# SBUF homes moved by small steps under a stream of float32r matmuls

## The chip, the cores and the metric

The kernel runs on one core of one Trainium2 chip. The metric is the device time of one execution in microseconds (us), the median of several runs. A profile of one execution stands beside it. The engines are called as the profile calls them: PE is the matrix engine (TensorE), PEld its weight loads, DVE the vector engine, ACT the scalar engine, POOL the general engine (GpSimd) and SP the queue that issues most transfers. SBUF is the on-chip memory: 128 partitions, and a tile's home is its byte offset, the same in all of them.

## The reference, cut to what matters

A residual of 256 tokens by 2048 features passes through five phases. Each takes `rms_norm(x) * gain`, multiplies it by weight matrices, does something in between, and adds the product of a last matrix to the residual:

```
x += mixer(norm(x))        # w_in [2048, 8272], gated recurrence + sparse attention, w_out [2048, 2048]
x += cross(norm(x), mem)   # wq, wk, wv [2048, 512], attention over 256 memory rows, wo [512, 2048]
x += relu(norm(x) @ w_up)**2 @ w_down          # w_up [2048, 8192], w_down [8192, 2048]
x += neighbourhood(norm(x))                    # w_qkv [2048, 6144], w_o [2048, 2048]
x += relu(norm(x) @ w1)**2 @ w2                # w1 [2048, 8192], w2 [8192, 2048]
```

All in float32. Some 440 MB of weights are each used once for the 256 tokens.

## The kernel before, in words

The program is one stream of weight chunks with side work beside it. A chunk is at most 1024 float32 columns in each partition: two 128-row tiles of a 512-column block (four of a 256-column block). For each, SP brings a `raw` tile (512 KB, `emit_dma`), ACT copies it to `hi` in float32r (L374), and DVE writes the rest, `raw - hi`, to `lo` (L375). Activations are split in two the same way. A product of two split numbers takes three matmuls: high by high, high by low, low by high. That is `emit_mm`, which has two forms:

- Transposed blocks (`tr=True`, line L408): the weights stand still (128 columns of `hi` or `lo`) and the activations stream past, 256 columns of `xT_hi` or `xT_lo`. These are the indexer's, gates' and up-projection blocks.
- Token blocks (L415, L416, L417): 128 columns of activations stand still and the weights stream past, 512 columns (256 for the value projection of the cross attention). The standing operand is `xT_hi`, `xT_lo` for projections of the residual, or a region tile (`r0` to `r8`) for projections of something made in between: squared-ReLU activations, attention outputs, the normalised memory rows.

```
nc.tensor.matmul(dst, h, wh, start=first, stop=False)   # L415: h, l stand still; wh, wl stream
nc.tensor.matmul(dst, h, wl, start=False, stop=False)   # L416
nc.tensor.matmul(dst, l, wh, start=False, stop=last)    # L417
```

The standing operand is always the second of the tiles that the program names for a matmul, and the streaming one the first: `acc<-hi,r` streams `hi` past a region tile. The order of all work is written out when the program is made: estimated clocks (`spend`, `Paced`) decide when a stage of side work goes between two chunks. They depend on operand sizes and not on homes.

Homes follow from the order in which the pools were opened (`const`, `stream`, `reg`, `tmp`, `small`) and from the tile sizes. Before the change: a scratch of 16384 bytes for the descriptors of POOL's transfers, four constants of 32 bytes each that the toolchain places, then `cst` 1024, `band` 256, `lvl` 896, `gT` 512, `X` 16384 bytes; so `xT_hi` and `xT_lo` (16384 bytes each) begin at 256 modulo 512. Small tiles after them add up so that `stream` begins at 32 modulo 512. Everything in `stream` (4 `raw`, 4 `hi`, 4 `lo` of 4096 bytes) and in `reg` (nine regions of 8192 bytes) has a size that is a multiple of 512, so all of these, and the wide working tiles in `tmp`, begin at 32 modulo 512. All slices that matmuls of the stream take begin at multiples of 512 bytes inside their tiles, except in one 80-column block.

Of the kernel before, what the change touches and what calls it, by code (L numbers as in the profile page):

```python
# [12 lines left out]
F32 = mybir.dt.float32  # L13
F32R = mybir.dt.float32r
# [8 lines left out]
P = 128  # L23
T = 256
# [9 lines left out]

# columns of the transposed table of gains
G_MIX, G_CROSS, G_MEM, G_MLP, G_MIX2, G_MLP2 = 0, 16, 32, 48, 64, 80
# [19 lines left out]
class Block:  # L56
    """One block of output columns: w[kts, cols] against the stationary activations."""

# [6 lines left out]
class Act:  # L65
    """Transposed activations, each value split exactly into two float32r parts."""

# [8 lines left out]
def block_kernel(ctx: ExitStack, tc: "_tile.TileContext", a: dict, out: bass.AP, phases=ALL_PHASES):  # L76
# [27 lines left out]
    def region(i, shape, dtype=F32):  # L104
        return reg.tile(shape, dtype, tag=f"r{i}", name=nm(f"r{i}"))

    # ------------------------------------------------------------------ lanes of side work
    # Work beside the stream of weights is written as generators, each in a lane. The estimated clocks
    # below only order the program: a stage goes out when the one before it should be done by the time
    # the tensor engine gets there, and when ACT and DVE aren't too far behind it.  # L110
    clock = {"pe": 0.0, "act": 0.0, "dve": 0.0, "pool": 0.0}
# [100 lines left out]

    # ------------------------------------------------------------------ constants
    cst = const.tile([P, 2 * P], F32, name="cst")
# [3 lines left out]
    gT = const.tile([P, P], F32, name="gT")  # L218
    X = const.tile([P, 2, D], F32, name="X")
    xT_hi = const.tile([P, KT, T], F32R, name="xT_hi")  # L220
    xT_lo = const.tile([P, KT, T], F32R, name="xT_lo")
# [10 lines left out]

    # ------------------------------------------------------------------ small arithmetic
    def rsqrt(lane, x, n, mul=1.0, out=None):
        """1/sqrt(x) * mul of a [P, n] tile: an integer first guess, then Newton's steps."""
        g = st(f"rg{lane}", n, I32)
        vec.tensor_scalar(g, x.bitcast(I32), 1, None, op0=ALU.logical_shift_right)
        vec.tensor_scalar(g, g, -1, RSQRT_MAGIC, op0=ALU.mult, op1=ALU.add)
        y = st(f"ry{lane}", n) if out is None else out
        h = st(f"rh{lane}", n)  # L240
        for i in range(3):
            y0 = g.bitcast(F32) if i == 0 else y
            m = mul if i == 2 else 1.0
            gps.tensor_tensor(h, y0, y0, op=ALU.mult)
            gps.tensor_tensor(h, h, x, op=ALU.mult)
            gps.tensor_scalar(h, h, -0.5 * m, 1.5 * m, op0=ALU.mult, op1=ALU.add)
            gps.tensor_tensor(y, h, y0, op=ALU.mult)
        return y
# [4 lines left out]
    def make_rstd(lane, key, ss, want_sq=False):  # L253
        """ss: [P, 2 * 4] sums of squares, one per token half and column block."""
        v = vec
        m = st(f"mr{lane}", 2)
        v.tensor_reduce(m, ss.rearrange("p (t c) -> p t c", t=2), axis=AX.X, op=ALU.add)
        ms = const.tile([P, 2], F32, name=nm("ms"))
        v.tensor_scalar(ms, m, 1.0 / D, EPS, op0=ALU.mult, op1=ALU.add)
        if want_sq:  # L260
            r2 = const.tile([P, 2], F32, name=nm("rsq"))
            v.reciprocal(r2, ms)
            rstd_sq[key] = r2
        else:
            rstd[key] = rsqrt(lane, ms, 2, out=const.tile([P, 2], F32, name=nm("rstd")))
        mark(("rstd", key))
# [3 lines left out]
    def build_half(lane, ver, cb, gain, half):  # L270
        """Two feature tiles of the finished residual: transposed, with the gain, split in two."""
        yield from wait_for(("x", ver, cb))
        act = acts[ver]
        ps = sd("E")
        for j in range(2):
            kt = cb * 4 + half * 2 + j
            for tt in range(2):
                pe.transpose(
                    ps[:, j * T + tt * P : j * T + (tt + 1) * P], X[:, tt, kt * P : (kt + 1) * P], ident
                )  # L280
        yield
        for j in range(2):
            kt = cb * 4 + half * 2 + j
            act.put(kt, xT_hi[:, kt, :], xT_lo[:, kt, :])
        kts = [cb * 4 + half * 2 + j for j in range(2)]
        split_gains([act.parts[kt] for kt in kts], ps, [gcol(gain + kt) for kt in kts])
        for kt in kts:
            mark(("act", id(act), kt))
        yield
# [25 lines left out]
    def split_act(hi, lo, src, scale=None):  # L315
        """hi + lo = src * scale, exactly; src in PSUM or SBUF."""
        if scale is None:
# [8 lines left out]
    def product(dst, l, r, first=True, last=True):  # L326
        """dst (+)= l^T r; operands split in two parts take three products."""
        if not isinstance(l, tuple):
# [9 lines left out]
    def split_gains(parts, ps, gains):  # L338
        """The same of two feature tiles in one PSUM bank, each with its own gain."""
        srcs = [ps[:, j * T : (j + 1) * T] for j in range(2)]  # L340
# [4 lines left out]

    # ------------------------------------------------------------------ the stream of weights
    plan = []
# [22 lines left out]
    def emit_split(c):  # L370
        n = len(c.kts) * c.block.width
        c.hi = stream.tile([P, 1024], F32R, tag="hi", name=nm("hi"))
        c.lo = stream.tile([P, 1024], F32R, tag="lo", name=nm("lo"))
        nc.scalar.activation(c.hi[:, :n], c.raw[:, :n], AF.Copy)  # L374
# [51 lines left out]

    # ------------------------------------------------------------------ evacuations
    def ev_tokens(dst, key, after=None):
        """dst[tt] = projection * rstd, one row per token."""
        def ev(b):  # L430
# [12 lines left out]
    def ev_heads(dstT, key, gain, after, mul=1.0, lane="E", factor=None):  # L443
        """Four heads of 128: RMS norm of each, transposed; dstT(pair) is [128, 2, 256].

        With factor, the norm is left to the scores: factor["ss"] holds the heads' sums of squares.
        """
        def ev(b):
# [60 lines left out]
    def softmax_rows(lane, groups, factor=None):  # L509
        """groups: (scores [P, n, w] in SBUF or PSUM, destination [P, n, w]); normalised rows.  # L510

        factor(group) is a [P, n] of positive factors that the scores still lack.
        """
        v = vec
# [70 lines left out]

    # ------------------------------------------------------------------ phase: mixer
    def mixer():
# [45 lines left out]

        # --- indexer
        iqT = region(0, [P, 8, T])
# [89 lines left out]

        # --- sparse attention heads
        qT = region(2, [P, 8, T])
# [68 lines left out]

        # --- gated recurrence heads
        hold = {}
# [77 lines left out]
        def levels(g, pl):  # L876
            """Scores of the recurrence, S^T[s, t] = sum_k q[t] k[s] prod(f, s < . <= t): pairs are met at
            the level where a block of 2b tokens holds s in its left and t in its right half; q carries the
            products from its half's start, k those to its half's end."""
            v = vec  # L880
# [46 lines left out]
            def right_pairs(b, ps):  # L927
                """The level's products, for the tokens in right halves alone."""
                for i in range(2):
# [93 lines left out]

    # ------------------------------------------------------------------ attention of dense heads
    def probs_pair(qT, kTt, h0, pT, keys, bias=None, lane="A", pl="A", factor=None):
        """Two heads: softmax(q k^T + bias), transposed into the two tiles pT()."""
        yield from wait_for(*keys)
# [41 lines left out]
    def values_pair(pT, V, vcol, oT_hi, oT_lo, oh, act_o, vkey):  # L1069
        """out^T of two heads from their transposed probabilities, split into the next operand."""  # L1070
        yield from wait_for(vkey)
# [12 lines left out]

    # ------------------------------------------------------------------ phase: cross attention
    def cross():
# [96 lines left out]

    # ------------------------------------------------------------------ phase: squared-ReLU MLP
    def mlp(phase, w1, w2):
# [45 lines left out]

    # ------------------------------------------------------------------ phase: neighbourhood attention
    def na():
# [83 lines left out]

    # ------------------------------------------------------------------ the program
    warm = st("warm", 8)
# [106 lines left out]
```

## Time and profile before

| | |
|---|---|
| median of 3 runs | 2477.0 us (2476.63 to 2477.68) |
| profiled execution, first to last instruction | 2475.9 us |
| PE busy | 2459.3 us, 99% of the span |
| PE weight loads busy | 2186.8 us, 88% |
| DVE, ACT, POOL busy | 1455.8, 1136.8, 169.5 us |
| moved by transfers | 449.40 MB, mean 182 GB/s |

The span is the time from the first to the last instruction of the profiled execution; the 1.1 us between it and the median lie around it. PE's instructions overlap one another in the profile (the recorded length of one is longer than the distance to the next), so what one matmul costs is read from the distance between starts, not from its length.

### The profile page before, as it was taken

How to read it: one execution, taken by the hardware profiler on the slowest of the kernel's cores; microseconds unless marked ns; L12 is line 12 of the kernel's file. 1: busy time of each engine (PE TensorE's matmuls, PEld its weight loads, DVE VectorE, ACT ScalarE, POOL GpSimd, SP SyncE). 2: the span in 40 equal slices, each digit the busy share in tenths (PEclk: the TensorE clock that was granted, in tenths of full speed). 3: DMA queues.
4: the chain of work that ended last, by engine and by line, in shares of the span. 5: the costliest groups of instructions: out<-in, count | busy, mean ns of one | idle time of the engine just before them, and what ended most of it. 6: DMA issues, size and time to landing. Idle time of an engine off the chain costs nothing.

```text
span 2475.9 us, 36932 instructions
## 1 busy us (share of the span) xinstructions
PE 2459.3 (99%) x14885; PEld 2186.8 (88%) x14885; DVE 1455.8 (59%) x1719; ACT 1136.8 (46%) x1465; POOL 169.5 (7%) x345
## 2 busy tenths in 40 slices
PE   8999999999999999999999999999999999999999
PEld 8779998888998899899898888888998899899897
DVE  5575666665655555555556566666655555555554
ACT  5455533465543444444444554554543444444443
POOL 1020012211000000000000312230000000000000
PEclk9999999999999999999999999999999999999999
DMA  7555545555556556566655656555556656566654
GB/s 225 162 172 161 151 145 156 193 177 167 170 178 198 193 182 194 187 194 191 189 187 174 196 169 179 167 186 180 179 180 195 195 180 196 188 194 188 190 187 167
DMA packets 235644, 449.40 MB, mean 182 GB/s; under 512 B 16321, under 2 KB 21057, under 8 KB 235473
## 3 DMA queue, kind: packets, MB, share of 16 engines
q1 hardware_dynamic: 232528, 440.19, 57.0%
q0 software_dynamic: 2368, 5.80, 1.0%
q8 instruction: 116, 1.90, 0.3%
q10 hardware_dynamic: 576, 1.05, 0.1%
q14 instruction: 56, 0.45, 0.1%
HBM read 444.83 MB, written 2.10 MB: 181 GB/s over the span
## 4 chain that ended last, share of the span: by engine, by line
PE 95%; POOL 1%; DMA 1%; DVE 1%; ACT 1%; issue 0%; SPq 0%; ACTq 0%; POOLq 0%; DVEq 0%
PE acc L408 34%; PE acc L415 19%; PE acc L416 19%; PE acc L417 19%; PE sdA L157 3%; PE sdE L157 2%; DMA raw<-in_w_in_dram 1%; DMA relraw<-in_rel_dram 0%; POOL rhB L157 0%; ACT hi L374 0%; DVE lo L375 0%; DMA wA<-in_mem_dram 0%; POOL rhD L157 0%; DVE wB L157 0%; POOL rhE L157 0%
## 5 line engine op out<-in xcount | busy, mean ns | idle before, releaser
L375 DVE TENSOR_TENSOR lo<-raw,hi 128x1024 fp32r<-128x1024 f32 (+1 forms) x835 | 1005.1, 1222 | 495.0 <-ACT hi L374 492.0
L374 ACT ACTIVATE hi<-raw 128x1024 fp32r<-128x1024 f32 (+1 forms) x835 | 867.7, 1056 | 799.5 <-PE acc L417 406.0
L408 PE MATMUL acc<-xT_hi,hi 128*128 128x256 f32 x2448 | 690.6, 282 | 0.0
L408 PE MATMUL acc<-xT_hi,lo 128*128 128x256 f32 x2448 | 688.3, 281 | 0.1
L408 PE MATMUL acc<-xT_lo,hi 128*128 128x256 f32 x2448 | 688.2, 281 | 0.0
L415 PE MATMUL acc<-hi,r 128*128 128x512 f32 (+1 forms) x1408 | 543.6, 386 | 0.7 <-ACT r L157 0.7
L417 PE MATMUL acc<-hi,r 128*128 128x512 f32 (+1 forms) x1408 | 541.5, 385 | 0.0
L416 PE MATMUL acc<-lo,r 128*128 128x512 f32 (+1 forms) x1408 | 541.4, 384 | 0.0
L408 PEld LDWEIGHTS acc<-xT_lo,hi 128*128 128x128 f32 x2448 | 461.2, 188 | 0.6
L408 PEld LDWEIGHTS acc<-xT_hi,hi 128*128 128x128 f32 x2448 | 461.2, 188 | 0.6
L408 PEld LDWEIGHTS acc<-xT_hi,lo 128*128 128x128 f32 x2448 | 461.2, 188 | 0.3 <-DVE lo L375 0.3
L417 PEld LDWEIGHTS acc<-hi,r 128*128 128x128 f32 x1408 | 264.5, 188 | 53.1 <-DVE r L157 0.4
L415 PEld LDWEIGHTS acc<-hi,r 128*128 128x128 f32 x1408 | 264.7, 188 | 52.3 <-ACT r L157 1.1
L416 PEld LDWEIGHTS acc<-lo,r 128*128 128x128 f32 x1408 | 264.7, 188 | 51.0
L415 PE MATMUL acc<-hi,xT_hi 128*128 128x512 f32 x736 | 295.0, 401 | 0.0
L416 PE MATMUL acc<-lo,xT_hi 128*128 128x512 f32 x736 | 290.9, 395 | 1.4 <-DVE lo L375 1.4
L417 PE MATMUL acc<-hi,xT_lo 128*128 128x512 f32 x736 | 290.5, 395 | 0.0
L157 DVE SCALAR_TENSOR_TENSOR X<-acc,rsq,X 128x512 f32<-128x512 f32 x128 | 96.1, 751 | 147.0 <-PE acc L417 147.0
L415 PEld LDWEIGHTS acc<-hi,xT_hi 128*128 128x128 f32 x736 | 138.1, 188 | 33.8 <-issue 2.7
L417 PEld LDWEIGHTS acc<-hi,xT_lo 128*128 128x128 f32 x736 | 137.9, 187 | 33.7
L416 PEld LDWEIGHTS acc<-lo,xT_hi 128*128 128x128 f32 x736 | 138.2, 188 | 32.7 <-DVE lo L375 1.9
L157 DVE SCALAR_TENSOR_TENSOR wE<-acc,wE 128x512 f32<-128x512 f32 x64 | 44.3, 692 | 109.2 <-ACT wE L157 108.6
(175 smaller groups left out, 1121.9 us busy)
## 6 DMA issues: line engine op xcount, KB each, us to landing
raw<-in_mlp_w_dram SPq DMA_DIRECT2D x256, 512.0 KB, 4.2
raw<-in_w_up_dram SPq DMA_DIRECT2D x128, 512.0 KB, 3.9
raw<-in_w_down_dram SPq DMA_DIRECT2D x128, 512.0 KB, 4.3
raw<-in_w_in_dram SPq DMA_DIRECT2D x127, 512.0 KB, 3.9
raw<-in_na_w_qkv_dram SPq DMA_DIRECT2D x96, 512.0 KB, 4.2
raw<-in_w_out_dram SPq DMA_DIRECT2D x32, 512.0 KB, 4.2
raw<-in_na_w_o_dram SPq DMA_DIRECT2D x32, 512.0 KB, 4.1
raw<-in_wk_x_dram SPq DMA_DIRECT2D x8, 512.0 KB, 4.4
```

Source lines behind the costliest of these rows:

```text
L157: return f(*args, **kw)
L374: nc.scalar.activation(c.hi[:, :n], c.raw[:, :n], AF.Copy)
L375: nc.vector.tensor_tensor(c.lo[:, :n], c.raw[:, :n], c.hi[:, :n], op=ALU.subtract)
L408: nc.tensor.matmul(dst, l, r, start=first and i == 0 and o == 0, stop=last and i == 2, skip_group_check=True,)
L415: nc.tensor.matmul(dst, h, wh, start=first, stop=False)
L416: nc.tensor.matmul(dst, h, wl, start=False, stop=False)
L417: nc.tensor.matmul(dst, l, wh, start=False, stop=last)
```

## The change: what it does

Four edits move homes; no instruction is added, taken away or reordered, and no operand changes its size.

- A tile of 32 bytes, `shift`, is put ahead of `xT_hi`.
- `hi` and `lo` tiles take 4160 bytes in place of 4096; the 1024 columns in use stay the same.
- Region `i` takes 8192 + 32 * i bytes; the part in use is a view on its first bytes.
- The descriptor scratch of POOL's transfers is 8192 bytes in place of 16384.

Beside them comments are dropped.

Modulo 512 bytes, the homes become:

| tile | before | after |
|---|---|---|
| `xT_hi`, `xT_lo` | 256 | 288 |
| `raw` | 32 | 64 |
| `hi`, four buffers | 32 | 64, 128, 192, 256 |
| `lo`, four buffers | 32 | 320, 384, 448, 0 |
| regions r0, r2, r3, r1, r4, r5, r8, r6, r7 (order of first use) | 32 | 64, 64, 128, 224, 256, 384, 32, 288, 480 |
| wide working tiles (`wA`, `wE`, `wB`) | 32 | 192 |

```diff
     def region(i, shape, dtype=F32):
-        return reg.tile(shape, dtype, tag=f"r{i}", name=nm(f"r{i}"))
+
+        flat = reg.tile([P, 2048 + 8 * i], dtype, tag=f"r{i}", name=nm(f"r{i}"))
+        n = 1
+        for d in shape[1:]:
+            n *= d
+        names = "abc"[: len(shape) - 1]
+        return flat[:, :n].rearrange(
+            f"p ({' '.join(names)}) -> p {' '.join(names)}", **dict(zip(names, shape[1:])))
...
     X = const.tile([P, 2, D], F32, name="X")
+    const.tile([P, 8], F32, name="shift")
     xT_hi = const.tile([P, KT, T], F32R, name="xT_hi")
...
-        c.hi = stream.tile([P, 1024], F32R, tag="hi", name=nm("hi"))
-        c.lo = stream.tile([P, 1024], F32R, tag="lo", name=nm("lo"))
+        c.hi = stream.tile([P, 1040], F32R, tag="hi", name=nm("hi"))
+        c.lo = stream.tile([P, 1040], F32R, tag="lo", name=nm("lo"))
...
-    nc = _bacc.Bacc("TRN2", target_bir_lowering=False, num_devices=1)
+    nc = _bacc.Bacc("TRN2", target_bir_lowering=False, num_devices=1, dynamic_dma_scratch_size=8192)
```

## Rows read from the trace of the kernel before

**Rows 1.** The page: busy time, share of the span and instructions of each engine.

```profile
PE 2459.3 (99%) x14885; PEld 2186.8 (88%) x14885; DVE 1455.8 (59%) x1719; ACT 1136.8 (46%) x1465; POOL 169.5 (7%) x345
```

**Rows 2.** The page: granted clock of PE in 40 slices, in tenths.

```profile
PEclk9999999999999999999999999999999999999999
```

**Rows 3.** The page: the chain that ended last, by engine, then by line.

```profile
PE 95%; POOL 1%; DMA 1%; DVE 1%; ACT 1%; issue 0%; SPq 0%; ACTq 0%; POOLq 0%; DVEq 0%
PE acc L408 34%; PE acc L415 19%; PE acc L416 19%; PE acc L417 19%; PE sdA L157 3%; PE sdE L157 2%; DMA raw<-in_w_in_dram 1%; DMA relraw<-in_rel_dram 0%; POOL rhB L157 0%; ACT hi L374 0%; DVE lo L375 0%; DMA wA<-in_mem_dram 0%; POOL rhD L157 0%; DVE wB L157 0%; POOL rhE L157 0%
```

**Rows 4.** Waits of PE: us in total, times, longest us.

```profile
PE sdE L157 <- DMA cst<-in_cst_dram: 2.9, 1, 2.9
PE sdA L157 <- DVE wA L157: 2.5, 3, 1.3
...
PE acc L416 <- DVE lo L375: 1.4, 1, 1.4
```

**Rows 5.** Groups of PE's instructions by form: count | busy us, mean ns of one.

```profile
L408 PE MATMUL acc<-xT_hi,hi 128*128 128x256 f32 x2432 | 686.2, 282 | 0.0
...
L415 PE MATMUL acc<-hi,r 128*128 128x512 f32 x1344 | 525.3, 391 | 0.7 <-ACT r L157 0.7
...
L415 PE MATMUL acc<-hi,xT_hi 128*128 128x512 f32 x736 | 295.0, 401 | 0.0
...
L415 PE MATMUL acc<-hi,r 128*128 128x256 f32 x64 | 18.3, 285 | 0.0
```

**Rows 6.** The chain, 860 to 1240 us: start us, us, what, how many.

```profile
869.62 45.44 PE acc L408 x384
...
958.62 45.44 PE acc L408 x384
...
1047.63 45.44 PE acc L408 x384
```

**Rows 7.** Timeline of PE, a token run of the first MLP: start us, us, instruction.

```profile
1003.90 0.40 PE L415 MATMUL acc<-hi,r 128*128 128x512 f32 x1
...
1005.99 0.39 PE L415 MATMUL acc<-hi,r 128*128 128x512 f32 x1
...
1006.67 0.39 PE L415 MATMUL acc<-hi,r 128*128 128x512 f32 x1
...
1047.24 0.39 PE L417 MATMUL acc<-hi,r 128*128 128x512 f32 x1
1047.47 0.28 PE L408 MATMUL acc<-xT_hi,hi 128*128 128x256 f32 x1
```

**Rows 8.** Timeline of PE, a token run of the neighbourhood projection.

```profile
1399.08 0.39 PE L416 MATMUL acc<-lo,xT_hi 128*128 128x512 f32 x1
...
1421.00 0.39 PE L417 MATMUL acc<-hi,xT_lo 128*128 128x512 f32 x1
```

**Rows 9.** Timeline of PE, the value projection of the cross attention.

```profile
592.05 0.28 PE L415 MATMUL acc<-hi,r 128*128 128x256 f32 x1
...
596.37 0.28 PE L415 MATMUL acc<-hi,r 128*128 128x256 f32 x1
```

**Rows 10.** Timeline of all engines at 1030 us: a matmul and the load beside it.

```profile
1030.02 0.39 PE L416 MATMUL acc<-lo,r 128*128 128x512 f32 x1
1030.02 0.19 PEld L417 LDWEIGHTS acc<-hi,r 128*128 128x128 f32 x1
```

**Rows 11.** The same at 1410 us.

```profile
1410.04 0.40 PE L415 MATMUL acc<-hi,xT_hi 128*128 128x512 f32 x1
1410.04 0.19 PEld L416 LDWEIGHTS acc<-lo,xT_hi 128*128 128x128 f32 x1
```

**Rows 12.** The view of transfers: issues, KB each, median us to landing.

```profile
relraw<-in_rel_dram POOLq DMA_DIRECT2D x32, 96.0 KB, 3.8
```

**Rows 13.** The chain, 1538 to 1560 us.

```profile
1544.60 0.61 POOL relraw L1272
1545.21 3.95 DMA relraw<-in_rel_dram
```

**Rows 14.** The page: the two split instructions, mean ns of one | idle before.

```profile
L375 DVE TENSOR_TENSOR lo<-raw,hi 128x1024 fp32r<-128x1024 f32 (+1 forms) x835 | 1005.1, 1222 | 495.0 <-ACT hi L374 492.0
L374 ACT ACTIVATE hi<-raw 128x1024 fp32r<-128x1024 f32 (+1 forms) x835 | 867.7, 1056 | 799.5 <-PE acc L417 406.0
```

## The prediction, made before the changed kernel was run

> **What bounds the kernel now.** I read the page first. PE is busy for 99% of the span [rows 1], at a granted clock that stays at the full level, 2.4 GHz, from the first slice to the last [rows 2]. The chain of work that ended last puts 95% on PE, and 91% on the four lines of the weight stream [rows 3]. The waits of PE agree: the longest is 2.9 us, for the first transfer of all, and the stream's longest is one of 1.4 us for a `lo` tile [rows 4]. So nothing but the distance from one matmul to the next sets the time, and the reader is to look at that distance alone.
>
> A table of groups can't show it: the mean lengths there (282, 391, 401 ns) run on under the next matmul [rows 5]. It has to be taken from stretches in which nothing comes between. There are four kinds, by shape and by where the two operands live:
>
> - Transposed, 256 columns of `xT` at 256 modulo 512 past weights at 32: 384 in 45.44 us, 118.3 ns each [rows 6].
> - Token, 512 columns of weights at 32 past region tiles at 32: from 1006.67 to 1047.24 us are 179 steps, 226.65 ns each. The first nine of the run, from 1003.90 to 1005.99, take 232 ns each; the run of 192 as a whole (1003.90 to 1047.47) 226.9 [rows 7].
> - Token, 512 columns of weights at 32 past `xT` at 256: 94 steps in 21.92 us, 233.2 ns each [rows 8].
> - Token, 256 columns of weights at 32 past region tiles at 32: 36 steps in 4.32 us, 120.0 ns [rows 9].
>
> Two things are to be seen. The second and the fourth kind differ only in columns, and 106.65 ns for 256 more columns is 0.4166 ns a column, one per tick of 2.4 GHz. So each matmul costs its columns and a toll: 226.65 - 213.3 = 13.3 ns, 120.0 - 106.7 = 13.3 ns, and by the same reckoning 233.2 - 213.3 = 19.9 ns for the third kind and 118.3 - 106.7 = 11.7 ns for the first. And the second and third kind have one shape, one count of weight loads (the next matmul's load begins with the matmul, [rows 10, 11]) and one engine clock, and yet stand 6.5 ns apart. What differs is which tiles meet: homes that are equal modulo 512 in the one, 224 apart in the other. The transposed run takes 45.44 us to the hundredth, three times out of three [rows 6], while ACT, DVE and the transfers fall on it differently each time; so the toll isn't made by them.
>
> The counts are 3 x 2432 transposed and 48 narrower ones like them (7,344), 3 x 1344 = 4,032 token with regions, 3 x 736 = 2,208 token with `xT`, and 3 x 64 = 192 narrow ones [rows 5]. The whole toll is 7,344 x 11.7 + 4,032 x 13.6 + 2,208 x 19.9 + 192 x 13.3 = 86 + 55 + 44 + 3 = 188 us, 13.6 ns per matmul, 7.6% of the span. That is the pot from which this change can take, and to which it can add: 1 ns of mean toll is 13.8 us.
>
> **The change part by part.** The 32-byte tile, the 64 bytes on each `hi` and `lo` and the 32 * i on each region issue nothing. Operands keep their shapes and the program its order, so instruction counts, waits and queues stay. What moves is which homes meet while a matmul streams and the next one's operand is loaded. Before, a meeting has one distance modulo 512 in each kind of run: 0, 224, or 288 for the transposed. After, the distance changes with each buffer: transposed runs meet at 288, 352, 416, 480 (with `hi`) and 32, 96, 160, 224 (with `lo`); the token runs with `xT` at the same set mirrored; those with regions at distances that depend on region and buffer. Of the region meetings, the equal homes that are now the rule become the exception: going through the four pairs of the MLP (r0 r1, r2 r3, r4 r5, r6 r7) against four `hi` and four `lo`, one in seven is still 0. And no run settles: a chunk has 12 token matmuls, and the run of rows 7 needed nine to fall from 232 to 226.65.
>
> The trace of before shows two distances for 512 columns and two for 256, and nothing of the others. So each kind is bounded by the two rows of its shape, and I take the middle, since the new distances lie on no row. Token with regions: bounds 226.65 and 233.2, middle 230.0; 4,032 x (230.0 - 226.9) = +12.5 us. Token with `xT`: the same middle; 2,208 x (230.0 - 233.2) = -7.1 us. Transposed: bounds 118.3 and 120.0, middle 119.15; 7,344 x 0.85 = +6.2 us. The narrow ones: 192 x (119.15 - 120.0) = -0.2 us. The sum is +11.4 us. With every kind at its lower row it is -1.0 - 14.5 + 0 - 0.3 = -16 us, at its upper row +25.4 + 0 + 12.5 + 0 = +38 us.
>
> The Trainium skill has a rule against any effect: the page "TensorE: Matmul & The Clock Gate", section "Step-by-step: what each phase is for", says that the streaming operand and the weight load have a read port each, so that loading the next tile's weights takes nothing from the running matmul. By it the sum would be 0; the trace here disagrees in so far as one shape runs at 226.65 and at 233.2 ns. The same page's section "Back-to-back issue gap" puts a lone warm matmul at N/2.4 + 2.5 ns, 215.8 and 109.2 here; if the whole toll above that went, an estimate by that page would be 150 us less, 2327 us, which no row here shows.
>
> The other parts cost nothing in the sum. ACT's copy and DVE's subtraction keep shapes and take 1,056 and 1,222 ns of the 2.7 us that 12 token matmuls last; they sit idle 800 and 495 us before these instructions [rows 14], so a few per cent on them is hidden. The smaller descriptor scratch touches POOL's queue alone: its main load is 32 bias transfers that land in 3.8 us [rows 12]. They lie on the chain in one place [rows 13]; should a later one have to wait there for an earlier landing, it is 3.95 us once, and elsewhere PE's stream covers it. I take 0.
>
> **The rivals.**
>
> *Separation pays.* Nine regions and eight stream buffers on their own offsets might keep the two readers out of each other's way, and the toll falls in every kind at once. For it: the toll does depend on the homes, and the kind with 224 between its homes pays the most, so some distances must be worse than others and a mixture of many need not be worse than today's. Against it: today's equal homes are the cheap case at 512 columns. Priced at the lowest toll of any row, 11.7 ns: 512 columns take 225.0 ns; 4,032 x (225.0 - 226.9) + 2,208 x (225.0 - 233.2) = -7.7 - 18.1 = -26 us, 2451 us. It decides as soon as the mean toll after falls under 13.6 ns; a toll 1 ns lower than any row gives another -14 us.
>
> *Nothing happens.* The homes modulo 512 aren't what sets the toll (the two token kinds also differ in which tiles they read and how far apart these are as a whole), and the new homes pay what the old did: 2477 us. For it: rows 7 and 8 are two points, no more. Against it: each kind would have to keep its own pace under a new distance.
>
> *Every meeting as dear as the dearest.* The 19.9 ns of rows 8 become the rule, for 256 columns too: 4,032 x 6.3 + 7,344 x 8.3 = 25 + 61 = +86 us, 2563 us. Against it: the transposed kind has a distance of 288, which is 224 the other way round, and pays only 11.7 ns.
>
> **How the numbers follow.** The sum is made against the span of 2475.9 us; the median of the runs, 2477.0, is 1.1 us more, and I set 11.4 on the median: 2488 us, slower by 0.5%. A measurement of this kernel can tell about 0.2%, 5 us, from no change. I give the forecast 0.40 (its own range 2482 to 2515), separation 0.36 (2430 to 2472), nothing 0.17, the dear case 0.07. So faster 0.36, no change 0.17, slower 0.47. The range from 2442 to 2512 leaves out the dear case, the last of the forecast's upper bound, and separation where it goes below 9 us under its price.
>
> **What the profile after would show.** PE's share and count stay; the chain stays on the stream's lines. The transposed runs of 384 take 45.8 us if the forecast is right, 45.44 or less under separation. The token run of 192 that took 43.57 us takes 44.2 us, and loses the even beat of 226 and 227 ns: a beat that changes from chunk to chunk, with the buffer. The token runs with `xT` become the one kind that is quicker, near 230 ns. I am wrong if the token runs with regions stay at or below 226.65 ns with their homes no longer equal: then equal homes were no advantage, and the sign of the sum turns on the transposed kind, half of all matmuls, for which the trace has only two rows 1.7 ns apart.

## The result: slower by 0.8%, all of it in the token runs with regions

| | before | after |
|---|---|---|
| median | 2476.8 us (2475.2 to 2477.7, 4 runs) | 2494.8 us (2494.1 to 2495.3, 4 runs) |
| ratio | | 1.0076, 95% interval 1.0064 to 1.0088 |
| profiled span | 2475.9 us | 2492.3 us |
| PE busy | 2459.3 us | 2477.6 us |

The page of the changed kernel has the same engines at the same work: instruction counts are equal, and the busy time of DVE, ACT and POOL moves by at most 1.5 us [rows 1 for before].

```profile
PE 2477.6 (99%) x14885; PEld 2186.4 (88%) x14885; DVE 1457.3 (58%) x1719; ACT 1136.4 (46%) x1465; POOL 169.8 (7%) x345
```

PE's busy time grew by 18.3 us, and its idle time (span less busy) fell from 16.6 to 14.7 us. So it is the pace of PE's matmuls again. The chain of the changed kernel, two of the 384-matmul transposed runs (start us, us, what), answers to [rows 6]:

```profile
782.29 45.37 PE acc L416 x384
872.14 45.32 PE acc L416 x384
```

They are a shade quicker than the 45.44 us of before: 118.0 to 118.1 ns in place of 118.3. (Line numbers have moved: L416 is the old L408, L423 to L425 are the old L415 to L417.) The timeline of PE in the changed kernel, first the token run of 192 that answers to [rows 7], from its first matmul to the next transposed one, then the run with `xT` of [rows 8]:

```profile
1007.26 0.40 PE L423 MATMUL acc<-hi,r 128*128 128x512 f32 x1
...
1051.83 0.28 PE L416 MATMUL acc<-xT_hi,hi 128*128 128x256 f32 x1
...
1407.15 0.39 PE L424 MATMUL acc<-lo,xT_hi 128*128 128x512 f32 x1
...
1429.09 0.39 PE L425 MATMUL acc<-hi,xT_lo 128*128 128x512 f32 x1
```

The first takes 44.57 us where it took 43.57: 232.1 ns a matmul in place of 226.9. The second takes 21.94 us for 94 steps, 233.4 ns, where it took 233.2. Multiplied out over the counts of [rows 5]: regions 4,032 x 5.2 = +21.0 us, `xT` 2,208 x 0.2 = +0.4 us, transposed 7,344 x -0.25 = -1.8 us, in all +19.6, against the 18.3 us that PE's busy time grew. The stretches shown speak for the whole: over all neighbouring matmuls of a kind in the two traces, the mean distance between starts goes from 227.6 to 232.7 ns with regions, from 236.1 to 235.9 with `xT`, and from 118.8 to 118.6 in the transposed kind.

POOL's smaller scratch cost nothing that can be seen. The waits of POOL in the changed kernel (us in total, times, longest) have its bias tiles waiting 43.4 us for their transfers; PE waits for none of them.

```profile
POOL relb L164 <- DMA relraw<-in_rel_dram: 43.4, 14, 4.8
```

### The profile page after: what moved, and what is told of

It reads as the page before. It is cut to its first block, busy times and chain, and to the rows that moved or that the text cites. A ratio compares the mean times of both kernels' runs of the same rounds, so it can differ in the third digit from the quotient of the medians.

```text
span 2492.3 us, 36932 instructions
## 1 busy us (share of the span) xinstructions
PE 2477.6 (99%) x14885; PEld 2186.4 (88%) x14885; DVE 1457.3 (58%) x1719; ACT 1136.4 (46%) x1465; POOL 169.8 (7%) x345
## 4 chain that ended last, share of the span: by engine, by line
PE 95%; POOL 1%; DVE 1%; ACT 1%; DMA 1%; issue 0%; SPq 0%; ACTq 0%; POOLq 0%; DVEq 0%
PE acc L416 33%; PE acc L423 19%; PE acc L425 19%; PE acc L424 19%; PE sdA L164 3%; PE sdE L164 2%; DMA raw<-in_w_in_dram 1%; DMA relraw<-in_rel_dram 0%; POOL rhB L164 0%; ACT hi L382 0%; DVE lo L383 0%; POOL rhD L164 0%; DVE wB L164 0%; DVE wA L164 0%; POOL rhE L164 0%
## 5 line engine op out<-in xcount | busy, mean ns | idle before, releaser
L416 PE MATMUL acc<-xT_hi,hi 128*128 128x256 f32 x2448 | 689.6, 282 | 0.0
L416 PE MATMUL acc<-xT_hi,lo 128*128 128x256 f32 x2448 | 687.8, 281 | 0.0
L416 PE MATMUL acc<-xT_lo,hi 128*128 128x256 f32 x2448 | 686.0, 280 | 0.0
L423 PE MATMUL acc<-hi,r 128*128 128x512 f32 (+1 forms) x1408 | 550.6, 391 | 0.7 <-ACT r L164 0.7
L424 PE MATMUL acc<-lo,r 128*128 128x512 f32 (+1 forms) x1408 | 547.7, 389 | 0.0
L425 PE MATMUL acc<-hi,r 128*128 128x512 f32 (+1 forms) x1408 | 547.6, 389 | 0.0
L416 PEld LDWEIGHTS acc<-xT_lo,hi 128*128 128x128 f32 x2448 | 461.5, 189 | 0.7
L416 PEld LDWEIGHTS acc<-xT_hi,hi 128*128 128x128 f32 x2448 | 460.4, 188 | 0.7
L416 PEld LDWEIGHTS acc<-xT_hi,lo 128*128 128x128 f32 x2448 | 459.9, 188 | 0.3 <-DVE lo L383 0.2
L425 PEld LDWEIGHTS acc<-hi,r 128*128 128x128 f32 x1408 | 264.6, 188 | 60.2 <-DVE r L164 0.4
L423 PEld LDWEIGHTS acc<-hi,r 128*128 128x128 f32 x1408 | 264.6, 188 | 58.5 <-ACT r L164 1.1
L423 PE MATMUL acc<-hi,xT_hi 128*128 128x512 f32 x736 | 295.3, 401 | 0.0
L425 PE MATMUL acc<-hi,xT_lo 128*128 128x512 f32 x736 | 291.1, 396 | 0.0
L423 PEld LDWEIGHTS acc<-hi,xT_hi 128*128 128x128 f32 x736 | 138.4, 188 | 33.5 <-issue 2.7
L425 PEld LDWEIGHTS acc<-hi,xT_lo 128*128 128x128 f32 x736 | 138.2, 188 | 33.5
```

The source lines that it names most:

```text
L416: nc.tensor.matmul(dst, l, r, start=first and i == 0 and o == 0, stop=last and i == 2, skip_group_check=True,)
```

## The experiments

Four theories are told apart. Theory 1: the distance between the home of the tile that stands still and that of the tile that streams sets the toll; in form a, the cheap beat needs one distance throughout, and only equal homes have it; in form b, it is the rotation of buffers that spoils it; in form c, only the distance modulo 256 counts, and it may alternate. Theory 2: each home's own alignment sets the toll. A distance below is the standing home less the streaming home, modulo 512 bytes. All of these kernels have the smaller scratch as well.

### The tile of 32 bytes and the smaller scratch alone

```diff
+    const.tile([P, 8], F32, name="pad_x")
     xT_hi = const.tile([P, KT, T], F32R, name="xT_hi")
...
+    nc = _bacc.Bacc("TRN2", target_bir_lowering=False, num_devices=1, dynamic_dma_scratch_size=8192)
```

> The kernel before with the 32-byte tile ahead of xT_hi and the smaller descriptor scratch alone: xT goes to 288, weight buffers and regions all to 64 modulo 512, so every distance between homes that meet is what it was. Theory 1 (the distance and its constancy set the toll): every kind of run keeps its pace (118.3, 226.65, 233.2 ns), 2477 us. Theory 2 (the homes themselves, each by its own alignment): paces move, some of the 18 us is here. If the scratch matters, it shows here as waits of POOL.

Measured: 2477.6 us against 2475.9 for the kernel before, ratio 1.0008 (0.9999 to 1.0017). Its timeline has the token run at the old length, 43.57 us:

```profile
1005.81 0.40 PE L416 MATMUL acc<-hi,r 128*128 128x512 f32 x1
...
1049.38 0.28 PE L409 MATMUL acc<-xT_hi,hi 128*128 128x256 f32 x1
```

All homes of the stream moved by 32 bytes and no pace did. Theory 2 falls, for this step at least, and the scratch is cleared.

### The region steps alone, and the buffer steps alone

```diff
# first kernel: the change's region() alone
+        flat = reg.tile([P, 2048 + 8 * i], dtype, tag=f"r{i}", name=nm(f"r{i}"))
...
# second kernel: the weight buffers alone
+        c.hi = stream.tile([P, 1040], F32R, tag="hi", name=nm("hi"))
+        c.lo = stream.tile([P, 1040], F32R, tag="lo", name=nm("lo"))
```

> The kernel before with the region steps alone (and the smaller scratch). A region then has one distance to all weight buffers, but its high and low halves have two different ones, so a run meets two distances in turn. Theory 1a (the cheap beat needs equal homes, or at least one distance throughout): token runs with regions go from 226.65 to about 232 ns, +18 to +21 us, all of the change's cost. Theory 1b (it is the rotation of the weight buffers that unsettles the runs): they settle again, at a pace of their own per region, within 5 us of 2477.

> The kernel before with the 64 bytes on each weight buffer alone (and the smaller scratch). Regions keep one home, the buffers have eight. Theory 1a and 1b both: the token runs with regions go to about 232 ns, +18 to +21 us; under theory 1a this and the region steps each cost nearly all by themselves and don't add up. The transposed runs stay within 1 ns of 118.3, the token runs with xT near 233.

Measured: 2497.3 us, ratio 1.0084 (1.0071 to 1.0098), and 2491.6 us, ratio 1.0063 (1.0049 to 1.0077). The same token run, first with the region steps, then with the buffer steps:

```profile
1008.68 0.39 PE L421 MATMUL acc<-hi,r 128*128 128x512 f32 x1
...
1053.15 0.28 PE L414 MATMUL acc<-xT_hi,hi 128*128 128x256 f32 x1
```

```profile
1006.08 0.40 PE L415 MATMUL acc<-hi,r 128*128 128x512 f32 x1
...
1050.42 0.28 PE L408 MATMUL acc<-xT_hi,hi 128*128 128x256 f32 x1
```

44.47 and 44.34 us: 231.6 and 230.9 ns a matmul. Each half of the change costs nearly the whole by itself, and together they cost no more than the dearer one: what is lost is one thing, the equal homes, and either step loses it. Form b, with settled runs where the buffers share one home, falls.

### Constant distances, but others

Two pads: xT on the home of the weight buffers, regions 64 bytes further.

```diff
+    reg.tile([P, 16], F32, tag="pad_r", name="pad_r")
...
     xT_lo = const.tile([P, KT, T], F32R, name="xT_lo")
+    const.tile([P, 56], F32, name="pad_s")
```

> Constant distances again, but others: xT gets the home of the weight buffers (distance 0 in place of 224 and 288), the regions stand 64 bytes past it (64 in place of 0). Theory 1a (equal homes are the cheap case at 512 columns): token runs with xT fall from 233.2 to 226.65 ns, -14 us; those with regions rise towards 232, +21 us; the transposed runs go from 118.3 to the 120.0 ns of the 256-column row with equal homes, +12.5 us; in all about 2496 us. Rival (any constant distance settles, whatever it is): regions stay near 226.65, 2475 us.

Measured: 2502.4 us, ratio 1.0106 (1.0092 to 1.0120). From the timeline, the token run with regions, then the one with `xT`:

```profile
1009.16 0.40 PE L417 MATMUL acc<-hi,r 128*128 128x512 f32 x1
...
1053.97 0.28 PE L410 MATMUL acc<-xT_hi,hi 128*128 128x256 f32 x1
...
1411.34 0.39 PE L418 MATMUL acc<-lo,xT_hi 128*128 128x512 f32 x1
...
1432.67 0.39 PE L419 MATMUL acc<-hi,xT_lo 128*128 128x512 f32 x1
```

and from the chain, the transposed run:

```profile
963.27 46.06 PE acc L410 x384
```

The two kinds changed places. Regions at 64 take 44.81 / 192 = 233.4 ns, `xT` at 0 takes 21.33 / 94 = 226.9 ns, and the transposed kind at 0 takes 119.9 ns, as the narrow token kind with equal homes did [rows 9]. So the pace goes with the distance and not with the tile, and a constant distance by itself isn't cheap. The time came 6 us over the expected one because 64 costs more than the 232 ns that was put in.

### Each kind on a distance of its own

From here on the weight tiles are 1152 columns wide, all on one home with `xT` and the regions (by the 224-byte tile `pad_s` of the kernel above), and each kind of block reads them from a column of its own. The three numbers (transposed, token with `xT`, other token) are the ones that differ between the kernels; four columns are 16 bytes.

```diff
-        c.hi = stream.tile([P, 1024], F32R, tag="hi", name=nm("hi"))
-        c.lo = stream.tile([P, 1024], F32R, tag="lo", name=nm("lo"))
+        b = c.block
+        o = 16 if b.tr else 0 if any(b.act is x for x in acts.values()) else 0
+        c.hi = stream.tile([P, 1152], F32R, tag="hi", name=nm("hi"))[:, o : o + n]
+        c.lo = stream.tile([P, 1152], F32R, tag="lo", name=nm("lo"))[:, o : o + n]
```

> Distances chosen for each kind: 0 for all 512-column runs (xT, weights and regions on one home), and 64 for the transposed runs, which take columns 16 to 1039 of wider weight tiles. From the run with xT at 0 and regions at 64: token runs with xT 227.5 ns (-13 us), with regions 226.9 (as before), transposed at the 116.6 ns that the narrow token run showed at 64 (-15 us). Theory 1a (the distance alone sets the pace of a kind): about 2448 us. Rival (the transposed kind has its own dependence, or the tile matters): the transposed runs stay at 118 to 120 ns, 2462 to 2475 us.

Measured: 2459.2 us, ratio 0.9931 (0.9918 to 0.9945): faster than both kernels. Token runs with `xT` take 21.32 us for 94 steps, 226.8 ns. From the chain:

```profile
951.24 45.23 PE acc L411 x384
```

The transposed kind takes 117.8 ns here, not 116.6. The 116.6 was an average over two paces that the narrow kind kept at this distance in the kernel with `xT` at 0 and regions at 64: 70 steps from 589.35 to 597.59 us take 117.7 ns each, and 47 steps from 600.58 to 605.93 us take 113.8. The long transposed runs have the slower of the two; the quicker one turns up in this kernel as well, near its start (last section).

> Constant distances, standing home less streaming home: transposed 128, token with xT 256, token with regions 384. Theory 1a (0 alone is cheap at 512 columns): both token kinds near 233.3 ns, about 2500 us if the transposed kind stays near 118. Rival (several distances are cheap, by multiples of 128): a token kind near 227. For the transposed kind no number is known; between 116 and 120 ns.

> Small constant distances: transposed 32, token with xT 480 (weights 32 past), token with regions 496 (weights 16 past). Theory 1a in its sharp form (only equal homes): both token kinds at 232 to 233 ns, about 2495 us. In its broad form (near 0 is as good as 0): both near 227, about 2455 us.

> Transposed 16, token with xT 448 (64 the other way than the run with regions at 64), token with regions 128. Theory 1a: both token kinds near 233.3 ns. Rival (the sign counts: which of the two reads ahead): one of them stays near 227. Transposed, in the sharp form, is already off the 120 ns of equal homes and near 117.

Measured, one execution each, so that the paces are to be read and not the times: 2492.2, 2495.1 and 2491.4 us. The timelines of the three, the token runs with regions (192 steps) and with `xT` (94 steps):

```profile
1006.14 0.39 PE L418 MATMUL acc<-hi,r 128*128 128x512 f32 x1
...
1050.76 0.28 PE L411 MATMUL acc<-xT_hi,hi 128*128 128x256 f32 x1
...
1405.92 0.40 PE L419 MATMUL acc<-lo,xT_hi 128*128 128x512 f32 x1
...
1427.23 0.39 PE L420 MATMUL acc<-hi,xT_lo 128*128 128x512 f32 x1
```

```profile
1008.27 0.39 PE L418 MATMUL acc<-hi,r 128*128 128x512 f32 x1
...
1052.75 0.28 PE L411 MATMUL acc<-xT_hi,hi 128*128 128x256 f32 x1
...
1407.96 0.39 PE L419 MATMUL acc<-lo,xT_hi 128*128 128x512 f32 x1
...
1429.88 0.39 PE L420 MATMUL acc<-hi,xT_lo 128*128 128x512 f32 x1
```

```profile
1005.61 0.40 PE L418 MATMUL acc<-hi,r 128*128 128x512 f32 x1
...
1050.23 0.28 PE L411 MATMUL acc<-xT_hi,hi 128*128 128x256 f32 x1
...
1405.32 0.39 PE L419 MATMUL acc<-lo,xT_hi 128*128 128x512 f32 x1
...
1426.83 0.40 PE L420 MATMUL acc<-hi,xT_lo 128*128 128x512 f32 x1
```

Regions: 232.4 ns at 384, 231.7 at 496, 232.4 at 128. `xT`: 226.7 ns at 256, 233.2 at 480, 228.8 at 448. In the chains, the transposed runs of 384 take 45.56 us at 128, 45.43 at 32 and 45.43 to 45.44 at 16. The sharp form holds on one side (16 bytes off the equal home already costs 5 ns), and fails on the other: 256 is as cheap as 0. With 384 as dear as 128 and 480 as dear as 224 [rows 8], that suggested form c, so two more kernels were made for it, and one for the transposed kind.

In the first, `o` is 16, 0 and 0, and the `lo` tiles are read 256 bytes (64 columns) further on than the `hi` tiles; in the second, `o` is 56, 0 and 64; in the third 24, 0 and 0.

> The run with transposed distance 64 and equal homes elsewhere, with one thing changed: every lo weight tile is read 256 bytes further on, so that in each run two distances alternate, 0 and 256 in the token runs, 64 and 320 in the transposed ones. Theory 1c (only the distance modulo 256 counts, and it may alternate between 0 and 256): all paces as in that run (226.9, 227.3, 118.0 ns), 2459 us. Theory 1a (one distance must stay): token runs at about 232 ns, 2490 us.

> Transposed 224, token with xT 0, token with regions 256. Theory 1c: regions at 256 keep the cheap pace, 226.9 ns, xT 227.3 ns; the transposed kind at 224 has not been seen with one distance throughout; the changed kernel's mixture suggests 116 to 118 ns. 2445 to 2460 us. If 256 is cheap for xT alone, regions go to 232 and the time to about 2475 us.

> Transposed 96, all token runs at 0. Token paces as in the run with transposed 64 (226.9, 227.3 ns). Transposed between 117 and 119 ns by its neighbours at 64 (118.0) and 128 (119.2); each 1 ns is 7.3 us; 2452 to 2467 us.

Measured, one execution each: 2461.2, 2454.5 and 2460.8 us. The timelines of the first and the second in the token run with regions, 43.55 us in both:

```profile
996.31 0.40 PE L418 MATMUL acc<-hi,r 128*128 128x512 f32 x1
...
1039.86 0.28 PE L411 MATMUL acc<-xT_hi,hi 128*128 128x256 f32 x1
```

```profile
994.88 0.40 PE L418 MATMUL acc<-hi,r 128*128 128x512 f32 x1
...
1038.43 0.28 PE L411 MATMUL acc<-xT_hi,hi 128*128 128x256 f32 x1
```

226.8 ns with 0 and 256 in turn, and the same with 256 alone. Form a falls: a distance may alternate, if it stays at 0 modulo 256. The transposed run of 384 takes 45.23 us with 64 and 320 in turn (as with 64 alone), 44.80 us at 224 and 45.06 us at 96.

### The best of these

```diff
+        o = 56 if c.block.tr else 48 if c.block.width == 256 else 0
```

> All 512-column runs at distance 0, transposed at 224, and the 192 narrow token matmuls with their weights read 192 bytes further on (distance -192, that is 64 modulo 256). Theory 1c: 226.9, 227.3, 117.1 ns as seen, and the narrow ones at the 116.6 ns that the distance 64 gave them, 0.8 us less in all: 2452 to 2455 us, a ratio near 0.991. If distances count modulo 512 and not 256 at 256 columns, the narrow ones come out elsewhere.

Measured: 2452.7 us against 2474.8, ratio 0.9912 (0.9895 to 0.9928): 22 us under the kernel before and 42 under the changed one. The chain has the transposed run at 116.7 ns. The timeline has the narrow kind at 320 (which is -192) with both paces of 64: 70 steps in 8.25 us, 117.9 ns, and 47 steps in 5.34 us, 113.6 ns.

```profile
948.14 44.80 PE acc L410 x384
```

```profile
583.45 0.28 PE L418 MATMUL acc<-lo,r 128*128 128x256 f32 x1
...
591.70 0.28 PE L419 MATMUL acc<-hi,r 128*128 128x256 f32 x1
...
594.69 0.29 PE L417 MATMUL acc<-hi,r 128*128 128x256 f32 x1
...
600.03 0.28 PE L419 MATMUL acc<-hi,r 128*128 128x256 f32 x1
```

Over all four of its runs the narrow kind averages the 116.6 ns that were expected, and the expected time held.

Put together, in ns per matmul, where one distance stood throughout (512 columns from token runs; 256 columns from the long transposed runs of 384):

| distance | 0 | 16 | 32 | 64 | 96 | 128 | 224 | 256 | 288 | 384 | 448 | 480 | 496 |
|---|---|---|---|---|---|---|---|---|---|---|---|---|---|
| 512 columns | 226.7 | | | 233.4 | | 232.4 | 233.2 | 226.7 | | 232.4 | 228.8 | 233.2 | 231.7 |
| 256 columns | 119.9 | 118.3 | 118.3 | 117.8 | 117.3 | 118.6 | 116.7 | | 118.3 | | | | |

## Why the prediction was right, and which terms were off

**What bounds the kernel.** Right: PE's share, counts and clock stayed, and the change is in the distance between matmuls. The 188 us of toll is a real pot: other homes take 22 us out of it.

**Token with regions.** The mechanism was right: equal homes were the cheap case and the change gives them up. The size was off: +12.5 us was forecast, from 230.0 ns, and 232.1 ns came, +21.0 us. The step that failed is "each kind is bounded by the two rows of its shape, and I take the middle, since the new distances lie on no row". The bounds held to 0.2 ns at 512 columns, the middle didn't: of nine distances tried at 512 columns, 0 and 256 lie at the lower row and all others at 228.8 to 233.4. As it came out, the better guide stood in the group that the term came from: the first nine matmuls of the run took 232 ns [rows 7], the pace that the changed kernel keeps throughout.

**Why it doesn't settle.** The prediction said that no run settles because a chunk has only 12 matmuls at one distance. That reason is too narrow: distances that alternate between 0 and 256 settle as well as one alone, and constant 64 or 128 never come down. What is lost is the cheap distance, not the constancy.

**Token with `xT`.** Wrong: -7.1 us and "the one kind that is quicker" were forecast by the same middle; +0.4 us came, 233.4 ns. The new distances were as dear as the old one.

**Transposed.** Wrong in sign: +6.2 us forecast, -1.8 us measured. The upper bound, the 120.0 ns of equal homes, was taken to be as near as the lower, and the lower, 118.3, was no bound: the changed kernel's 118.0 to 118.1 lies under it. At 256 columns equal homes are the dear case, and every other distance on the list is at or under 118.6 ns. A forecast of the same sum with 232 ns for both token kinds and no change for the transposed would have been +21 - 3 = +18 us, as measured; what brought the 11.4 as near as it is was luck: the transposed term was some 8.0 us too high, and the two token terms some 8.5 and 7.5 us too low.

**The parts set at nothing.** Right: the scratch, POOL's transfers and the two split instructions moved nothing that can be seen. (The bias transfers lie on the chain of before in one stretch, but twice in it, at 1545.21 us for 3.95 us and at 1551.18 us for 4.90 us.)

**The rivals.** "Nothing happens" falls by the run in which `xT` and the regions exchange their paces with their distances. "As dear as the dearest" came nearly true at 512 columns (232.1 and 233.4 ns) and not at 256. "Separation pays" is false for these offsets, but its price of 2451 us is what the best of the experiments reached, 2452.7, by the opposite of separation in the token runs: equal homes there, and a distance of 224 in the transposed ones.

The Trainium skill's rule that loading the next tile's weights takes nothing from the running matmul ("TensorE: Matmul & The Clock Gate", "Step-by-step: what each phase is for") would have given 0. The runs disagree with the 0: the same instructions on the same tiles run at 233.2 or 226.9 ns as 224 bytes of padding are put between them. Whether they disagree with the rule itself is open: that the partner of the streaming tile is the load of the next matmul's weights is argued from the overlap in [rows 10, 11], and no run here takes the load away, so it isn't shown. (The tolls above that page's 2.5 ns add up to 153 us by the prediction's own figures, not 150; nothing else rests on it.)

## What to carry to other kernels

When PE's stream has no waits left, read the distance between starts in stretches without anything in between, for each pair of standing and streaming tile, and compare pairs of one shape: a difference there was a matter of homes here, and pads or shifted columns of 16 to 384 bytes told it, one run per set of distances. Don't spread homes out on principle: the best distance differs by shape (0 or 256 for 512 float32r columns, 224 among those tried for 256), and one wider tile can serve two shapes by being filled and read from a different column. If an unknown price is bounded by two rows, ask which of them is the exception before taking the middle.

## What the runs showed of the hardware that was not expected

The pace of float32r matmuls, each with its own weight load, depends on the distance of two homes; at 512 columns, as far as tried, on the distance modulo 256 bytes, and sharply: 226.7 ns at 0 and 256, 231.7 ns 16 bytes away. Steps of whole 512 bytes don't show: within a run the buffers and slices that meet lie different multiples of 512 bytes apart, and the pace of [rows 7] stays at 226.65 ns for 179 steps.

At 256 columns one distance can have more than one beat. In the kernel with the distances 32, 480 and 496 the narrow token runs stand at 496, and two of its runs, in the timeline, keep different paces: 7.94 us for 70 steps, 113.4 ns, and 5.58 us for 47 steps, 118.7 ns.

```profile
592.57 0.28 PE L419 MATMUL acc<-lo,r 128*128 128x256 f32 x1
...
600.51 0.28 PE L420 MATMUL acc<-hi,r 128*128 128x256 f32 x1
...
603.50 0.28 PE L418 MATMUL acc<-hi,r 128*128 128x256 f32 x1
...
609.08 0.28 PE L420 MATMUL acc<-hi,r 128*128 128x256 f32 x1
```

The same holds at 64: 117.9 and 113.6 ns for the narrow kind in the best kernel above, and, in the kernel with the transposed kind at 64 and equal homes elsewhere, 113.3 ns for 99 transposed steps near its start against 117.8 in its long runs:

```profile
26.66 0.28 PE L411 MATMUL acc<-xT_lo,hi 128*128 128x256 f32 x1
...
37.88 0.28 PE L411 MATMUL acc<-xT_lo,hi 128*128 128x256 f32 x1
```

So the distance alone doesn't fix the pace at 256 columns. How a run is entered may be what picks it, but no run varies that alone. That also leaves open whether 256 columns go by the distance modulo 256: of the narrow runs at 384 (in the kernel with the distances 128, 256 and 384), one has 70 steps in 8.40 us, 120.0 ns, and another 47 steps in 5.58 us, 118.7 ns, where the transposed ones at 128 take 118.6.

```profile
588.82 0.29 PE L419 MATMUL acc<-lo,r 128*128 128x256 f32 x1
...
597.22 0.29 PE L420 MATMUL acc<-hi,r 128*128 128x256 f32 x1
...
600.21 0.28 PE L418 MATMUL acc<-hi,r 128*128 128x256 f32 x1
...
605.79 0.28 PE L420 MATMUL acc<-hi,r 128*128 128x256 f32 x1
```

Some 113.3 ns is the lowest steady pace seen at this shape. If the transposed kind kept it throughout, its 7,344 matmuls would take some 25 us less than in the best kernel here, an estimate from 116.7 and 113.3 ns; at 64, where it was seen, it didn't last, and at 496 the transposed kind wasn't tried. What makes the beats is open.
